# Making the low half of streamed weights with an accumulating transfer in the second mixer of a hybrid decoder trunk

## The chip, the cores and the metric

The kernel runs on one core of a Trainium2 chip. The metric is the device time of one launch in microseconds (us), lower is better. The engines of a core have one instruction queue each, worked off in order: TensorE (PE) multiplies matrices, VectorE (DVE) and ScalarE (ACT) work on 128 rows at a time, GpSimd (POOL) does small work, SyncE (SP) issues transfers. Transfers (DMA) run beside them on 16 engines. Waits between queues go over semaphores.

## The reference, cut to what matters

A trunk of two layers works on x of [1, 512, 1024] in float32. Each layer is a half feed-forward network, a mixer, and another half feed-forward network, each followed by a normalisation. The second layer's mixer, which the change touches, has RWKV-7 heads and gated linear attention (GLA) heads, one input projection and one output projection:

```python
def reference(x, ...):
    for l in range(DEPTH):                       # DEPTH = 2
        x = layer_norm(alpha * x + 0.5 * swiglu_ffn(x, ffn1_wi[l], ffn1_wo[l]), ...)
        mix = even_mixer(x, ...) if l % 2 == 0 else odd_mixer(x, ...)
        x = layer_norm(alpha * x + mix, ...)
        x = layer_norm(alpha * x + 0.5 * swiglu_ffn(x, ffn2_wi[l], ffn2_wo[l]), ...)

def odd_mixer(x, w_in, w_out, ...):
    p = x @ w_in
    y_rk = rwkv7_mixer(p[..., :RK_IN], ...)      # r, k, v, three small low-rank inputs
    y_gla = gla_mixer(*split_cols(p[..., RK_IN:], GLA_SIZES), ...)   # q, k, v, gate, output gate
    return jnp.concatenate([y_rk, y_gla], axis=-1) @ w_out

def rwkv7_mixer(p, ...):
    kk = heads(k * k_k)
    kk = kk / jnp.maximum(jnp.sqrt(jnp.sum(kk * kk, -1, keepdims=True)), 1e-12)   # the key norm
    def step(state, inp):                        # a scan over 512 tokens, 8 heads of 64
        sa = einsum(state, -kk_t)
        state = state * w_t + sa * (kk_t * a_t) + v_t * k_t
        return state, einsum(state, r_t)
    return (head_norm(y, ...) + (r * k * r_k).sum(-1) * v) * g
```

## The kernel before

**Three matmuls for one.** Every large product x @ w is made of three passes in a rounded 32-bit format (float32r): x is split into xh + xl and w into whi + wlo, and the kernel adds xh*whi, xl*whi and xh*wlo into one PSUM tile. In `project_T_steps` these are L122, L123 (the sixteen "high" matmuls of a chunk) and L126 (its eight "low" ones, after all high ones); in the GLA projections L146 to L148, in the feed-forward networks and the output projection L155 to L157.

**Streaming weights.** Weights come from HBM in chunks of 512 KB, a [128, 1024] float32 tile: 128 rows of 4 KB. `load` (L86) is SP's transfer into one of two `raw` tiles. `split` makes the halves in two pieces of 512 columns: ScalarE's copy rounds `raw` into `whi` (L98), VectorE subtracts: `wlo` = `raw` - `whi` (L100). There are five `whi` and five `wlo` tiles, taken in turn; a tile comes free when PE has read its last column of the chunk five earlier. `weights()` is called when a chunk's projection begins, splits up to two chunks ahead, and asks for two more loads.

**The second mixer** (`odd`) uses 34 chunks: a low-rank input and a gate, then twelve for k, r, v of four groups of heads (named k0, r0, v0, k1, ... below), four for the GLA q and k, four for v, four for the output gate, and eight for the output projection (`MixOut`). Its steps:

- k0, r0, v0 and the two small projections are made for the first 256 tokens; then the last quarter of x is transposed on PE (`pst`, L168) and the other 256 tokens follow.
- `keys` prepares a group of heads: a squared key (ScalarE, L690) summed by PE (`pn`), its floor on VectorE (L696), the power -0.5 on POOL (`nrm`, L697), a broadcast on ScalarE (L717), four transposes on PE (`pi`, L719), the scaled key on VectorE (L721) and products after it. VectorE's L744 masks the scores (`psc`) and ScalarE's L753 copies transposed keys (`KV`).
- `inverse` inverts 32 triangular blocks at a time by substitution: a chain of some sixty small VectorE operations (`ZU`, L782 and L783), ended by the 32x32 transposes L786 and L789. `merge` joins the blocks: PE's `pq` (L800) reads L786's result `WT`, ScalarE and VectorE copy `pq` (L802), PE's `px` (L807) reads that, L809 copies it, and `pwt`, `pu` (L822) follow. This comes twice, for head groups 0, 1 and 2, 3.
- The GLA heads' output gate `po` is scaled on VectorE by L958 and L959.

**What sets the order.** The program is written as Python that a scheduler reads: it simulates the engines, and puts each engine's instructions in the order of its own simulated times. Between the small steps, `fill()` takes matmuls of the projections that wait in a list (`filler`), as many as the table `FILL` gives for that place. An operation added or taken out in one place can so change the order on other engines.

## Time and profile before

| what | us |
|---|---|
| time, median of 3 runs | 2059.55 (2056.95 to 2061.2) |
| the profiled execution's own time | 2057.05 |
| its span (first to last instruction) | 2055.3 |
| TensorE busy | 2014.7 |
| VectorE busy | 1002.1 |
| ScalarE busy | 687.5 |
| GpSimd busy | 68.5 |
| mean granted TensorE clock | 0.983 |

Rows of the views are read so: in a group of instructions stand line, engine, operation, the tile written and the tiles read, shape and count, then the busy time with the mean in ns, then the engine's idle time just before and what ended most of it. A row of the timeline has its start, its length, engine, line, operation, tiles, shapes, count, and in brackets how long the engine stood idle before it and whose end released it. A window row has its bounds and length, then the busy time and count of each engine, the granted clock (1.00 is full), the busy share of the transfer engines, and GB/s. Matmuls overlap, so a matmul's length is more than the step from one to the next.

The second mixer lies between about 1329 and 1685 us. In the page's 40 slices of 51.4 us, TensorE is under nine tenths in four: two from 1387 to 1490 us, one from 1541 to 1593 us, and the last.

### The profile page before, as it was taken

The numbers are of one execution on the slowest core, as the hardware profiler recorded it, in microseconds if no ns is written. First come the engines' busy times: TensorE is split into PE (matmuls) and PEld (weight loads), VectorE is DVE, ScalarE is ACT, GpSimd is POOL, SyncE is SP. The second block draws the span as 40 slices with busy tenths as digits, with TensorE's granted clock in tenths as the row PEclk, the third lists the DMA queues.
The fourth block names the chain that finished last, engine by engine and source line by source line (L and its number), as shares of the span: only waits on it lengthen the run. The fifth ranks groups of instructions, "written<-read, shape, count | busy, mean of one in ns | idle before, by whom it ended". The sixth has DMA issues, their size and how long they took to land.

```text
span 2055.3 us, 26008 instructions
## 1 busy us (share of the span) xinstructions
PE 2014.7 (98%) x10485; PEld 1670.5 (81%) x10485; DVE 1002.1 (49%) x1858; ACT 687.5 (33%) x1206; POOL 68.5 (3%) x128
## 2 busy tenths in 40 slices
PE   9999999999999999999999999998898999999998
PEld 8888888977888888888888888886777688888886
DVE  4332333766783323336332333678758684323335
ACT  4331331556423322332332233255223334322330
POOL 0000000100010000000000000000010210000001
PEclk9999999999999999999999999998898999999999
DMA  5233332322233233332333333241113023333331
GB/s 176 93 102 113 103 93 82 107 92 62 66 100 113 92 102 114 101 95 72 113 92 103 113 98 97 86 140 40 59 31 114 1 74 119 95 97 118 94 102 62
DMA packets 56456, 191.42 MB, mean 93 GB/s; under 512 B 7488, under 2 KB 7952, under 8 KB 56336
## 3 DMA queue, kind: packets, MB, share of 16 engines
q1 hardware_dynamic: 56336, 189.77, 29.4%
q8 instruction: 82, 1.34, 0.3%
q14 instruction: 38, 0.31, 0.0%
HBM read 185.55 MB, written 4.19 MB: 92 GB/s over the span
## 4 chain that ended last, share of the span: by engine, by line
PE 90%; DVE 7%; ACT 1%; DMA 1%; issue 1%; POOL 0%; POOLq 0%; DVEq 0%; SPq 0%; ACTq 0%
PE pgu L122 16%; PE pgu L123 16%; PE pgu L126 16%; PE acc L157 8%; PE acc L155 8%; PE acc L156 8%; PE pout L155 1%; PE pout L156 1%; PE pout L157 1%; DVE wlo L100 1%; PE pj L122 1%; PE pj L123 1%; PE pj L126 1%; PE pst L168 1%; DVE ZU L782 1%; DVE ZU L783 1%
## 5 line engine op out<-in xcount | busy, mean ns | idle before, releaser
L100 DVE TENSOR_TENSOR wlo<-raw,whi 128x512 fp32r<-128x512 f32 x658 | 426.4, 686 | 549.6 <-ACT whi L98 513.2
L98 ACT ACTIVATE whi<-raw 128x512 fp32r<-128x512 f32 x661 | 379.6, 623 | 841.8 <-PE pgu L123 401.2
L122 PE MATMUL pgu<-xh,whi 128*128 128x512 f32 (+1 forms) x1568 | 563.1, 368 | 1.5 <-ACT whi L98 1.3
L123 PE MATMUL pgu<-xl,whi 128*128 128x512 f32 (+1 forms) x1568 | 564.0, 368 | 0.0
L126 PE MATMUL pgu<-xh,wlo 128*128 128x512 f32 (+1 forms) x1568 | 353.6, 367 | 0.0
L122 PEld LDWEIGHTS pgu<-xh,whi 128*128 128x128 f32 x1568 | 294.1, 188 | 50.4 <-ACT whi L98 1.5
L123 PEld LDWEIGHTS pgu<-xl,whi 128*128 128x128 f32 x1568 | 295.3, 189 | 48.6
L126 PEld LDWEIGHTS pgu<-xh,wlo 128*128 128x128 f32 x1568 | 275.8, 189 | 48.6
L155 PE MATMUL acc<-whi,hh 128*128 128x512 f32 x704 | 274.4, 390 | 0.0
L156 PE MATMUL acc<-whi,hl 128*128 128x512 f32 x704 | 274.2, 389 | 0.0
L157 PE MATMUL acc<-wlo,hh 128*128 128x512 f32 x704 | 272.3, 390 | 0.0
L233 DVE TENSOR_TENSOR sg<-sg,pgu 128x512 f32<-128x512 f32 (+1 forms) x96 | 61.6, 642 | 334.2 <-PE pgu L126 330.5
L156 PEld LDWEIGHTS acc<-whi,hl 128*128 128x128 f32 x704 | 132.2, 188 | 27.3
L157 PEld LDWEIGHTS acc<-wlo,hh 128*128 128x128 f32 x704 | 132.2, 188 | 27.2
L155 PEld LDWEIGHTS acc<-whi,hh 128*128 128x128 f32 x704 | 132.2, 188 | 27.0
L160 ACT ACTIVATE hh<-sg 128x512 fp32r<-128x512 f32 (+1 forms) x96 | 57.3, 597 | 120.9 <-DVE sg L233 120.9
L232 ACT ACTIVATE sg<-pgu 128x512 f32<-128x512 f32 (+1 forms) x96 | 53.7, 561 | 55.6 <-PE pgu L126 54.9
L160 ACT ACTIVATE xh<-pst 128x512 fp32r<-128x512 f32 x48 | 27.6, 598 | 108.5 <-PE pst L168 108.5
L122 PE MATMUL pj<-xh,whi 128*128 128x512 f32 (+2 forms) x184 | 63.5, 364 | 0.0
L190 POOL TENSOR_SCALAR rs<-mv 128x1 f32<-128x1 f32 x24 | 13.1, 547 | 1507.8 <-DVE mv L188 1507.8
L123 PE MATMUL pj<-xl,whi 128*128 128x512 f32 (+2 forms) x184 | 62.0, 354 | 0.0
L161 DVE TENSOR_TENSOR hl<-sg,hh 128x512 fp32r<-128x512 f32 (+1 forms) x96 | 61.5, 640 | 0.6 <-ACT hh L160 0.5
(336 smaller groups left out, 1968.6 us busy)
## 6 DMA issues: line engine op xcount, KB each, us to landing
raw<-ffn_wi SPq DMA_DIRECT2D x176, 512.0 KB, 3.5
raw<-ffn_wo SPq DMA_DIRECT2D x88, 512.0 KB, 3.5
raw<-od_krv SPq DMA_DIRECT2D x12, 512.0 KB, 3.5
raw<-ev_qk SPq DMA_DIRECT2D x8, 512.0 KB, 3.6
raw<-ev_rg SPq DMA_DIRECT2D x8, 512.0 KB, 3.5
raw<-ev_w_out SPq DMA_DIRECT2D x8, 512.0 KB, 3.5
raw<-od_w_out SPq DMA_DIRECT2D x8, 512.0 KB, 3.5
x<-x SPq DMA_DIRECT2D x4, 512.0 KB, 5.7
```

What stands on the lines that cost most here:

```text
L98: self.nc.scalar.activation(hi[:, sl], t[:, sl], AF.Copy)
L100: self.nc.vector.tensor_tensor(out=lo[:, sl], in0=t[:, sl], in1=hi[:, sl].bitcast(F32), op=ALU.subtract)
L122: mm(o, hi[:, kt, :n], self.xh[:, kt, t0:t1], start=kt == 0, stop=False)
L123: mm(o, hi[:, kt, :n], self.xl[:, kt, t0:t1], start=False, stop=lo is None and kt == 7)
L126: mm(o, lo[:, kt, :n], self.xh[:, kt, t0:t1], start=False, stop=kt == 7)
L155: mm(o, ah, hi[:, cs], start=first and i == 0, stop=False)
L156: mm(o, al, hi[:, cs], start=False, stop=False)
L157: mm(o, ah, lo[:, cs], start=False, stop=last and i == len(lhs) - 1)
L160: self.nc.scalar.activation(hi, src, AF.Copy)
L161: self.nc.vector.tensor_tensor(out=lo, in0=src, in1=hi.bitcast(F32), op=ALU.subtract)
L232: nc.scalar.activation(sg, pp[f, 0][:, t0:t1], AF.Silu)
L233: nc.vector.tensor_tensor(out=sg, in0=sg, in1=pp[u][:, t0:t1], op=ALU.mult)
```

## The change

From the start of `odd` until just before the mixer's last step, `split` makes `wlo` in another way. ScalarE makes two copies of each piece of 512 columns: the rounded `whi` as before, and `wlo` = -round(`raw`), a Copy with scale -1. POOL then issues a transfer that reads the chunk again from HBM and adds it to `wlo` in place (`accum_op`), so `wlo` = chunk - round(chunk), as before. SP's load into `raw` stays, since ScalarE reads it.

It holds for 29 chunks of this mixer: twelve of k, r, v, four each of GLA q and k, v, and output gate, and the first five of the output projection. The low-rank input was split before, the gate is of another kind (`fold`, its low part is packed in `whi`), and the last three of the output projection are split after the flag is off; these stay on VectorE. So 58 VectorE operations (L100) go, and 58 ScalarE operations and 29 transfers come.

```diff
--- before.py
+++ after.py
@@ -52,6 +52,7 @@
         self.srcs = []
         self.nl = self.nsp = self.nu = 0
         self.raw = {}
+        self.adds = False
         self.spl = {}
 
     def start(self):
@@ -84,20 +85,25 @@
         n = shape[0] * shape[1]
         t = self.wp.tile([P, 1024], F32, name="raw", bufs=NRAW)
         self.nc.sync.dma_start(t[:, :n].rearrange("p (a b) -> p a b", a=shape[0]), ap)
-        self.raw[self.nl] = (t, n, shape, fold)
+        self.raw[self.nl] = (t, n, shape, fold, ap)
         self.nl += 1
 
     def split(self):
         while self.nl <= self.nsp:
             self.load()
-        t, n, shape, fold = self.raw.pop(self.nsp)
+        t, n, shape, fold, ap = self.raw.pop(self.nsp)
         hi = self.wp.tile([P, 1024], F32R, name="whi", bufs=NSLOT)
         lo = None if fold else self.wp.tile([P, 1024], F32R, name="wlo", bufs=NSLOT)
         for z in range(0, n, 512):
             sl = slice(z, min(n, z + 512))
             self.nc.scalar.activation(hi[:, sl], t[:, sl], AF.Copy)
-            if not fold:
+            if self.adds and not fold:
+                self.nc.scalar.activation(lo[:, sl], t[:, sl], AF.Copy, scale=-1.0)
+            elif not fold:
                 self.nc.vector.tensor_tensor(out=lo[:, sl], in0=t[:, sl], in1=hi[:, sl].bitcast(F32), op=ALU.subtract)
+        if self.adds and not fold:
+
+            self.nc.gpsimd.dma_start(lo[:, :n].rearrange("p (a b) -> p a b", a=shape[0]), ap, accum_op=ALU.add)
         t, hi, lo = (z if z is None else z[:, :n].rearrange("p (a b) -> p a b", a=shape[0]) for z in (t, hi, lo))
         if fold:
             o = hi[:, :, fold:]
@@ -555,6 +561,7 @@
     def odd(self, l):
         nc, a, tc = self.nc, self.a, self.tc
         V, A, T, G = nc.vector, nc.scalar, nc.tensor, nc.gpsimd
+        self.adds = True
         xs = tc.alloc_tile_pool(name="xd", bufs=1, space=bass.MemoryType.DRAM).tile([S, D], F32, name="xs")
         for t in range(4):
             nc.sync.dma_start(xs[t * P:(t + 1) * P], self.x[:, t])
@@ -1100,6 +1107,7 @@
             for q in later:
                 rk_values(*q)
             gp.release()
+            self.adds = False
             mix.last(l, lambda nm: slot("y" if nm != "lnt" else "kr"))
 
 
```

The order moves with it. Line numbers of the changed kernel are one higher from L87 on, six higher after `split`, and seven higher in `odd`. On POOL, at the beginning of the mixer, before (`half`, `wk`: constants; `nrm`: the key norm):

```order
L191 TENSOR_TENSOR rs<-rs,expo 128x1
L587 MEMSET half 128x1
L620 MEMSET wk 80x512
L702 MEMSET wk 128x8
L697 TENSOR_TENSOR nrm<-nrm,expo 128x8
```

and now:

```order
L197 TENSOR_TENSOR rs<-rs,expo 128x1
L106 DMA wlo<-od_krv 128x1024
L594 MEMSET half 128x1
L106 DMA wlo<-od_krv 128x1024 x2
L627 MEMSET wk 80x512
L106 DMA wlo<-od_krv 128x1024 x3
L709 MEMSET wk 128x8
L106 DMA wlo<-od_krv 128x1024 x3
L704 TENSOR_TENSOR nrm<-nrm,expo 128x8
```

Nine transfers stand ahead of the first key norm, which had only constants before it.

On PE, the projections of the first 256 tokens, before (`pj_9945` is r0, `pj_9954` v0, `wlo_9920` the low part of r0; `pst` the transposes of x):

```order
L122 MATMUL pj_9945<-xh_71,whi_9919 128x256
L123 MATMUL pj_9945<-xl_72,whi_9919 128x256
L126 MATMUL pj_9945<-xh_71,wlo_9920 128x256 x4
L168 MATMUL pst_10067<-ident_73,x_70 128x128 x2
...
L168 MATMUL pst_10074<-ident_73,x_70 128x128 x4
L122 MATMUL pj_9954<-xh_71,whi_9928 128x256
```

and now (`pj_9939` and `wlo_9911` are k0, `pj_9949` r0, `pj_9959` v0):

```order
L128 MATMUL pj_9949<-xh_71,whi_9920 128x256
L129 MATMUL pj_9949<-xl_72,whi_9920 128x256
L174 MATMUL pst_10072<-ident_73,x_70 128x128 x4
L174 MATMUL pst_10079<-ident_73,x_70 128x128 x4
...
L128 MATMUL pj_9959<-xh_71,whi_9930 128x256
L129 MATMUL pj_9959<-xl_72,whi_9930 128x256
L132 MATMUL pj_9939<-xh_71,wlo_9911 128x256 x8
```

The transposes now stand among the high matmuls of r0, and k0's low matmuls, which came right behind its own high ones, stand behind half of v0's high ones. Those of r0 come later still, behind the second half of the low-rank projection.

On VectorE, the end of the second inverse, before (`og` is the output gate):

```order
L784 MEMSET ZU 64x32
L100 TENSOR_TENSOR wlo<-raw,whi 128x512
L783 TENSOR_TENSOR ZU<-ZU 64x2x29
...
L782 TENSOR_TENSOR ZU<-ZU 64x30
L958 SCALAR_TENSOR_TENSOR og_12118<-og_12118,po 128x512
L783 TENSOR_TENSOR ZU<-ZU 64x30
L959 TENSOR_TENSOR og_12118<-og_12118,cst 128x512
L786 STREAM_TRANSPOSE WT<-ZU 32x32x32
L789 STREAM_TRANSPOSE SC<-ZU 32x32x32 x2
L802 COPY WT<-pq 32x16x32
```

and now:

```order
L791 MEMSET ZU 64x32
L790 TENSOR_TENSOR ZU<-ZU 64x2x29
L789 TENSOR_TENSOR ZU<-ZU 64x30
L790 TENSOR_TENSOR ZU<-ZU 64x30
L793 STREAM_TRANSPOSE WT<-ZU 32x32x32
L796 STREAM_TRANSPOSE SC<-ZU 32x32x32 x2
L965 SCALAR_TENSOR_TENSOR og_12144<-og_12144,po 128x512
L966 TENSOR_TENSOR og_12144<-og_12144,cst 128x512
L809 COPY WT<-pq 32x16x32
```

No low part of weights is left in the chain of `ZU`, and the scaling of the output gate has moved behind the transposes.

## The prediction

> **What bounds the kernel now.** I read the page first: the span, TensorE's busy share and its 40 slices. Then the windows, cut where TensorE's idle time begins and ends, then the waits inside them.

> ```profile
> span 2055.3 us, 26008 instructions
> PE 2014.7 (98%) x10485; PEld 1670.5 (81%) x10485; DVE 1002.1 (49%) x1858; ACT 687.5 (33%) x1206; POOL 68.5 (3%) x128
> PE   9999999999999999999999999998898999999998
> L100 DVE TENSOR_TENSOR wlo<-raw,whi 128x512 fp32r<-128x512 f32 x658 | 426.4, 686 | 549.6 <-ACT whi L98 513.2
> q1 hardware_dynamic: 56336, 189.77, 29.4%
> raw<-od_krv SPq DMA_DIRECT2D x12, 512.0 KB, 3.5
> ```

> TensorE (PE) bounds the whole: 98% busy, and full in all slices but the last and three between 1387 and 1593 us (51.4 us each), which is the second mixer. The change touches only that mixer. The next rows are its stretches, all engines (us and count), then granted clock, DMA share and GB/s:

> ```profile
> 1331.00:1387.00 56.00, 56.00 (x369) 48.43 (x368) 40.47 (x72) 32.39 (x56) 3.70 (x8) 1.00 0.44 140
> 1387.00:1482.00 95.00, 82.69 (x635) 63.17 (x634) 76.79 (x140) 41.38 (x69) 5.76 (x7) 0.87 0.17 53
> 1533.00:1590.00 57.00, 49.88 (x450) 40.73 (x448) 46.50 (x93) 21.56 (x39) 1.07 (x4) 0.88 0.28 93
> ```

> The order is PE, weight loads, VectorE (DVE), ScalarE (ACT), GpSimd (POOL). In 1331-1387 PE never idles: whatever makes it wait there adds in full. In 1387-1482 PE idles 95.00-82.69 = 12.3 us, and VectorE is busy 76.79 of 95 us (81%). In 1533-1590 PE idles 7.1 us beside a VectorE that is 82% busy. In both, the clock is below full.

> Of VectorE's time, the low parts of weights (L100 alone, same stretches) take:

> ```profile
> 1387.00:1482.00 95.00, 11.79 (x18) 0.87 0.17 53
> 1533.00:1590.00 57.00, 8.13 (x12) 0.88 0.28 93
> ```

> **The change, term by term.** For 29 chunks of this mixer, 58 VectorE subtractions of 0.69 us go; 58 ScalarE copies and 29 accumulating transfers issued by POOL come. SP's loads stay.

> *Term 1, the first low parts (a loss).* The first three chunks (k0, r0, v0) arrive just before they are used, in the stretch where PE is full:

> ```profile
> 1332.14 2.38 ACT L98 ACTIVATE whi<-raw 128x512 fp32r<-128x512 f32 x4 [0.97 <-DMA raw<-od_krv]
> 1334.17 0.28 PE L122 MATMUL pj<-xh,whi 128*128 128x256 f32 x1
> 1334.29 0.28 PE L123 MATMUL pj<-xl,whi 128*128 128x256 f32 x1
> 1339.45 0.38 PE L168 MATMUL pst<-ident,x 128*128 128x128 f32 x2
> 1363.32 1.08 PE L126 MATMUL pj<-xh,wlo 128*128 128x512 f32 x4
> ```

> Four copies take 2.38 us. The two high and two negated ones of k0 are then done at 1332.14+2.38 = 1334.5 and its transfer can go. The new order reads k0's low part behind k0's and r0's high matmuls (16 each), 8 transposes and 8 high matmuls of v0: 40 x 0.12 (1334.29-1334.17) + 8 transposes at about 0.14 (two in under 0.38, less their overlap) = 5.9 us after 1334.17, so 1340.1. The transfer has 5.6 us.

> No row shows an accumulating transfer. The nearest is a plain load of the same 512 KB, 3.5 us: the lower bound. Splitting it: q1 is 29.4% of 16 engines x 2055.3 us over 56,336 packets = 0.172 us a packet; 128 rows of 4 KB are 8 packets an engine = 1.4 us of moving, so 2.1 us are fixed. Reading two operands makes the moving 2.8, reading and writing one after the other 4.2; with the fixed part 4.9 to 6.3, and POOL's issue, at most its slowest row below (1.65), makes 5 to 8. For the upper bound I double the slowest plain load:

> ```profile
> DMA to landing us min/median/max: 3.3/3.5/6.8
> ```

> 13.6 us. Against 5.6 us of room the cost is 0 (3.5) to +8 (13.6); a gain is excluded, since no PE wait is removed here. I take 7 us, nearest to the two-operand rows: 7 - 5.6 = 1.4, and **+2** with r0 and v0 behind it.

> [...]

> *Term 2, the key norm behind POOL's queue (a loss).*

> ```profile
> 1367.70 1.65 POOL L697 TENSOR_TENSOR nrm<-nrm,expo 128x8 f32<-128x8 f32 x1 [23.30 <-DVE nrm L696]
> 1369.38 0.63 ACT L717 ACTIVATE wk<-nrm 128x512 f32<-128x512 f32 x1 [1.48 <-POOL nrm L697]
> 1372.20 0.60 PE L719 MATMUL pi<-ident,wk 128*128 128x128 f32 x4
> 1389.40 1.98 PE L126 MATMUL pj<-xh,wlo 128*128 128x512 f32 x8
> ```

> In the new order POOL issues nine transfers ahead of this norm. The ninth waits for ScalarE's negated copy, that one for a low buffer (five of them), held until PE has read the fourth chunk's low part. From the fifth chunk's at 1363.32 PE has 8+15+11+8 = 42 matmuls at about 0.23 (1.98/8 with the overlap) and 4 small ones (1 us) to there: 1374.0. Then two copies 1.15, an issue of about 1, the norm 1.65, ScalarE's broadcast 0.63: 1378.4. PE reaches the waiting transposes (pi) 11 matmuls after that read, at 1376.5. So about 2 us, with 0.9 (issue free) to 4 (issue as long as the slowest POOL row, and term 1's delay added): **+2.5**. Queued behind pi on PE are the score matmuls of the first group, and on ScalarE, which waits at the broadcast, the next high parts.

> [...]

> *Term 3, the first VectorE-bound stretch (a gain).*

> ```profile
> 1391.47 1.29 DVE L100 TENSOR_TENSOR wlo<-raw,whi 128x512 fp32r<-128x512 f32 x2 [5.03 <-PE pj L126]
> 1395.33 1.33 PE L908 MATMUL pl<-ga,gw 80*128 80x512 f32 x2 [1.86 <-DVE wk L721]
> 1409.97 1.11 PE L752 MATMUL ptk<-ident,KRV 128*128 128x128 f32 x4 [1.39 <-DVE SC L744]
> 1426.55 0.97 PE L758 MATMUL ptb<-ident,bk 128*128 128x128 f32 x4 [1.61 <-ACT KV L753]
> 1475.01 1.76 PE L822 MATMUL pwt<-SC,KV 64*64 64x64 f32 x28 [2.70 <-DVE SC L809]
> 1445.36 1.98 PE L126 MATMUL pj<-xh,wlo 128*128 128x512 f32 x8
> ```

> VectorE stood 5.03 us behind a low part that waited for a buffer, with the scores' masks and L721 queued after it, and PE then waited for L721. That low part is first read at 1445.36, over 50 us later: the transfer is hidden here. VectorE gets 11.79 us of work and the 5.03 back. PE's idle time, 12.3 us, caps the gain, with a little clock above it. Waits on VectorE fall; the one on ScalarE (1.61) stays, and ScalarE gets 18 copies of about 0.57 (10 us), in a stretch where it is 44% busy. A bit over half of the cap: **-7** (-2 to -12). If ScalarE's copies stood ahead of its score copies the gain would end at -2.

> *Term 4, the end of the second inverse (a gain).*

> ```profile
> 1568.14 0.39 PE L148 MATMUL po<-wlo,xh 128*128 128x512 f32 x1
> 1573.32 1.81 PE L800 MATMUL pq<-WT,SC 32*32 32x32 f32 x64 [4.79 <-DVE WT L786]
> 1577.77 1.91 PE L807 MATMUL px<-SC,WT 32*32 32x32 f32 x62 [1.66 <-DVE WT L802]
> 1567.70 0.69 DVE L100 TENSOR_TENSOR wlo<-raw,whi 128x512 fp32r<-128x512 f32 x1
> 1570.55 0.69 DVE L959 TENSOR_TENSOR og<-og,cst 128x512 f32<-128x512 f32 x1
> 1571.28 1.90 DVE L786 STREAM_TRANSPOSE WT<-ZU 32x1024 f32<-32x1024 f32 x1
> 1577.02 0.69 DVE L802 COPY WT<-pq 32x512 f32<-32x512 f32 x1
> 1585.39 0.63 PE L148 MATMUL po<-wlo,xh 128*128 128x512 f32 x1
> 1585.82 0.63 PE L146 MATMUL po<-whi,xh 128*128 128x512 f32 x1
> ```

> PE waits 4.79 us for the transpose L786, the end of VectorE's substitution chain, into which ten of L100's twelve operations are laced (10 x 0.71 = 7.1 us), with the output scaling L958/L959 (1.4). All leave: L786 would come at 1571.28-8.5 = 1562.8, before PE's own filler ends at 1568.5. So pq starts at 1568.5 instead of 1573.32. The three transposes end at 1562.8+5.7 = 1568.5 too; the new order then puts the scaling (1.4) ahead of L802, so L802 runs at about 1570.8 and px at 1571.6 instead of 1577.77: -6. The matmuls here go at half pitch (0.43 between the last two rows, 0.23 elsewhere); a shorter gap gives back part of 12 x 0.2 = 2.4. **-7.5** (-3, if the fillers end as late as before and ScalarE's new copies hold the other half of WT, to -10).

> In 1482-1533 PE is nearly full, and after 1590 only two of the changed operations are left: 0, hidden behind PE.

> **Sum:** +2 + 2.5 - 7 - 7.5 = **-10 us**. The profiled execution took 2057.05 us, so 2047; it lies 2.5 under the median shown, 2059.55, on which basis I predict 2049.5.

> **The rivals.**
> *The transfers pace the start (slower).* Should the accumulating transfers run one behind the other at E us each, PE has five to read by 1363.32, from 1334.5: 28.8/5 = 5.8 us each. At E = 10 the fifth lands at 1384.5, 21 us late: +21+2.5-14.5 = +9, so 2068.5. It decides from 5E-28.8+2.5 = 14.5, E = 8.2. For it: no row shows this kind of transfer, and 13.6 is in bounds. Against it: moving 1.4 us, even three times, is far below. 0.13.
> *In-order waits eat the gains (a little slower).* POOL's later norms and ScalarE's copies stand behind transfers and buffers as in term 2; the 5.03 us wait moves to ScalarE, ahead of its projection copies. Three more waits like +2.5 and half of terms 3 and 4 (-7): +4.5+7.5-7, some +5, so 2064.5. For it: four key groups pass through POOL. Against: after the first, low buffers come free long before the norm. 0.10.
> *VectorE's time turns into other waits (no change).* ScalarE's score copies and PE's own order then set the pace: terms 3 and 4 give -3 each, +4.5 against: about -2, 2057.5. For it: waits on ScalarE stand between those on VectorE. 0.20.
> *More gain.* Both gaps close fully, with the clock back, and terms 1 and 2 cost nothing: -18, 2041.5. 0.05.

> **How the numbers follow.** The forecast, -16 to -4, has 0.52. A measurement tells 0.2% (4.1 us) from no change. Faster: 0.49 of the forecast, 0.05 of more gain, 0.03 of the no-change case = 0.57. Same: the other 0.17 and 0.02 of the forecast = 0.19. Slower: 0.13+0.10 and 0.01 over = 0.24. The range, 2037 to 2066, takes in more gain (beyond it terms 3 and 4 at their ends), no change and the in-order waits, and leaves out the pacing beyond +6.5; the forecast's own is 2043.5 to 2055.5.

> **What would show it.** Term 1: a wait of 1 to 3 us by PE for a DMA at k0's first low matmul, and POOL-issued transfers that land in 5 to 8 us. Term 2: the norm some 8 us later and a wait of pi for it. Term 3: no 5 us wait of VectorE near 1391, and PE idle some 5 to 6 us in the stretch that had 12.3. Term 4: PE's wait at pq under 1 us. Wrong if transfers land one after another more than 8 us apart, if PE's idle time in 1387-1482 stays over 10 us, or if ScalarE becomes the releaser of most PE waits.

## The result: faster, by more than forecast

The changed kernel took 2036.51 us (median of 4 runs, 2035.31 to 2039.38) beside 2059.5 for the kernel before: a ratio of 0.9893, 95% interval 0.9879 to 0.9907, 23 us faster. The forecast was 2049.5, its range 2037 to 2066; the time lies half a microsecond under it. The profiled execution took 2039.38 us, 17.7 less than that of before. A second series of the same kernel, below, was slower than the first (2046.26), and that is part of the explanation.

The page of the changed kernel, in the same parts as before:

```profile
span 2037.6 us, 26047 instructions
PE 2003.2 (98%) x10485; PEld 1661.1 (82%) x10485; DVE 966.1 (47%) x1800; ACT 716.7 (35%) x1264; POOL 95.1 (5%) x157
PE   9999999999999999999999999998999999999998
L103 DVE TENSOR_TENSOR wlo<-raw,whi 128x512 fp32r<-128x512 f32 x600 | 388.4, 687 | 533.4 <-ACT whi L99 507.8
q0 software_dynamic: 4176, 15.21, 4.0%
raw<-od_krv SPq DMA_DIRECT2D x12, 512.0 KB, 4.6
wlo<-od_krv POOLq DMA_DIRECT2D x12, 512.0 KB, 7.6
```

58 subtractions have left VectorE. The new transfers are the queue q0; those of k, r, v land 7.6 us after their issue in the median. PE has the same 10,485 matmuls, but is busy 11.5 us less, and its mean granted clock is 0.991 instead of 0.983: the same work ran at a higher clock.

**Where the time went.** I cut the mixer at five places of PE's program: the first low matmul of the projections (pj), the first of the GLA values (pv), the first of the output gate (po), the end of the last po that reads weights, the first of the output projection (pout). The windows, before and then changed (columns as in the prediction):

```profile
1331.33:1494.83 163.50, 151.16 (x1079) 120.53 (x1078) 123.03 (x233) 77.10 (x131) 11.12 (x18) 0.92 0.25 78
1494.83:1545.19 50.36, 48.84 (x298) 38.63 (x297) 31.93 (x92) 13.37 (x30) 6.38 (x16) 0.90 0.15 43
1545.19:1588.00 42.81, 35.69 (x343) 28.90 (x343) 33.81 (x68) 14.99 (x27) 0.00 (x0) 0.84 0.32 111
1588.00:1632.12 44.12, 40.03 (x433) 29.82 (x433) 29.91 (x105) 14.08 (x35) 8.35 (x20) 0.88 0.04 14
```

```profile
1330.94:1492.15 161.21, 149.52 (x1078) 119.11 (x1077) 97.81 (x193) 96.89 (x171) 29.92 (x38) 0.95 0.61 145
1492.15:1537.91 45.76, 44.23 (x297) 35.30 (x296) 28.12 (x87) 17.44 (x38) 8.66 (x16) 1.00 0.39 87
1537.91:1574.96 37.05, 35.29 (x343) 28.24 (x342) 27.56 (x57) 19.22 (x35) 4.50 (x8) 0.86 0.75 193
1574.96:1614.49 39.53, 35.86 (x434) 27.07 (x434) 29.37 (x103) 15.46 (x38) 9.23 (x21) 1.00 0.12 28
```

Call them stages 1 to 4. They changed by -2.3, -4.6, -5.8 and -4.6 us. Stages 1 and 3 hold everything that the forecast costed (terms 1 to 3, and 4): -8.1 against -10. Stages 2 and 4, which it put at zero, gave another -9.2. In both PE's idle time (length less busy) is about as before, 1.5 us in stage 2, and 4.1 and 3.7 us in stage 4; its clock is 1.00 where it was 0.90 and 0.88.

**What the clock does.** In stage 2 stands one and the same wait in both kernels:

```profile
1513.36 0.29 PE L840 MATMUL psa<-St,WT 128*64 128x128 f32 x1 [1.29 <-DVE St L852]
```

```profile
1510.68 0.29 PE L847 MATMUL psa<-St,WT 128*64 128x128 f32 x1 [1.29 <-DVE St L859]
```

Windows of PE alone around it, before and changed (length, PE busy, granted clock):

```profile
1512.07:1515.49 3.42, 2.13 (x18) 1.00 0.00 0
1515.49:1518.90 3.41, 3.41 (x18) 0.50 0.00 0
1518.90:1522.31 3.41, 3.41 (x21) 0.50 0.02 5
1522.31:1525.73 3.42, 3.42 (x11) 0.50 0.00 0
1525.73:1529.14 3.41, 3.41 (x25) 1.00 0.39 130
```

```profile
1506.74:1510.15 3.41, 2.65 (x16) 1.00 0.88 184
1510.15:1513.57 3.42, 2.89 (x21) 1.00 0.03 6
1513.57:1516.98 3.41, 3.41 (x35) 1.00 0.02 5
```

**What a half-clock field costs.** All executions of a kernel have the same instructions, yet 79 of the kernel before spread from 2050.6 to 2069.1 us, and their time follows their mean granted clock (correlation -0.89). Over all kernels here a clock lower by 0.001 goes with 1.61 us more; one field, half of 3.41 us at full clock lost, takes 1.71 of some 2056 us off the mean, 0.00083, so **1.34 us a field** on average (an estimate from these figures). Stage 2 shows it directly. PE idles 1.52 or 1.53 us in it in all seventeen traces, and its length is 45.7 to 45.8 us in the seven without a half-clock field, 48.8 in the two with two, 50.3 to 50.4 in the four with three, 51.9 in the four with four: 1.5 us a field where PE is otherwise busy, whatever the kernel. With the slope of 1.61 each kernel's mean difference to before splits into work and clock (us; an estimate, since one slope stands for all kernels):

| kernel | runs | mean us | mean clock | work | clock |
|---|---|---|---|---|---|
| before | 79 | 2058.5 | 0.982 | 0 | 0 |
| changed, first series | 4 | 2036.9 | 0.992 | -6.0 | -15.6 |
| changed, second series | 8 | 2044.7 | 0.988 | -4.6 | -9.1 |
| low parts from k1 on | 10 | 2036.9 | 0.991 | -8.4 | -13.2 |
| 17 later chunks | 10 | 2048.7 | 0.985 | -6.1 | -3.7 |
| nine k, r, v chunks | 10 | 2052.6 | 0.986 | +0.7 | -6.6 |
| six chunks of the second inverse | 10 | 2057.4 | 0.982 | -2.4 | +1.3 |
| no transfers | 9 | 2043.1 | 0.987 | -8.2 | -7.2 |

### The profile page after: what moved, and what is told of

It is laid out like the page before. It is cut to its first block, busy times and chain, and to the rows that moved or that the text cites. A ratio compares the mean times of both kernels' runs of the same rounds, so it can differ in the third digit from the quotient of the medians.

```text
span 2037.6 us, 26047 instructions
## 1 busy us (share of the span) xinstructions
PE 2003.2 (98%) x10485; PEld 1661.1 (82%) x10485; DVE 966.1 (47%) x1800; ACT 716.7 (35%) x1264; POOL 95.1 (5%) x157
## 3 DMA queue, kind: packets, MB, share of 16 engines
q1 hardware_dynamic: 56336, 189.77, 29.8%
q8 instruction: 82, 1.34, 0.3%
## 4 chain that ended last, share of the span: by engine, by line
PE 90%; DVE 4%; ACT 3%; DMA 2%; issue 1%; POOL 0%; POOLq 0%; SPq 0%; DVEq 0%; ACTq 0%
PE pgu L128 16%; PE pgu L129 16%; PE pgu L132 16%; PE acc L163 8%; PE acc L162 8%; PE acc L161 8%; PE pout L161 1%; PE pout L162 1%; PE pout L163 1%; DMA raw<-od_krv 1%; PE pv L152 1%; PE pst L174 1%; PE pj L128 1%; ACT whi L99 1%; PE pv L154 1%
## 5 line engine op out<-in xcount | busy, mean ns | idle before, releaser
L103 DVE TENSOR_TENSOR wlo<-raw,whi 128x512 fp32r<-128x512 f32 x600 | 388.4, 687 | 533.4 <-ACT whi L99 507.8
## 6 DMA issues: line engine op xcount, KB each, us to landing
raw<-ffn_wi SPq DMA_DIRECT2D x176, 512.0 KB, 3.5
raw<-ffn_wo SPq DMA_DIRECT2D x88, 512.0 KB, 3.5
raw<-od_krv SPq DMA_DIRECT2D x12, 512.0 KB, 4.6
wlo<-od_krv POOLq DMA_DIRECT2D x12, 512.0 KB, 7.6
raw<-ev_qk SPq DMA_DIRECT2D x8, 512.0 KB, 3.5
raw<-ev_rg SPq DMA_DIRECT2D x8, 512.0 KB, 3.4
raw<-ev_w_out SPq DMA_DIRECT2D x8, 512.0 KB, 3.5
raw<-od_w_out SPq DMA_DIRECT2D x8, 512.0 KB, 4.2
```

The source lines that it names most:

```text
L103: self.nc.vector.tensor_tensor(out=lo[:, sl], in0=t[:, sl], in1=hi[:, sl].bitcast(F32), op=ALU.subtract)
```

## The experiments

In the first, second and some later ones only the range of chunks changes for which the transfer is used (counted from the mixer's first chunk):

```diff
+        adds = self.adds and not fold and (self.nsp - self.base >= 5)
...
-            if self.adds and not fold:
+            if adds:
```

**The first three low parts on VectorE again** (range: 5 and up).

> The first three chunks (k0, r0, v0) get their low part from VectorE again; the other 26 keep the accumulating transfer. Theory S (the sum by stages: the mixer's beginning up to the k, r, v chunks' end lost 4.6 us, of which the late first low parts are a part): the wait of 2.1 us for k0's transfer and the half-clock window behind it go, so 3 to 5 us faster than the changed kernel, about 2032. Rival (the loss is the transfer engines' load and ScalarE's longer queue, which 26 chunks still bring): no change against the changed kernel, 2036 to 2038.

2034.17 us, ratio 0.9887 (0.9859 to 0.9916): between the two forecasts. Its first stage:

```profile
1333.87:1485.03 151.16, 144.36 (x1079) 115.87 (x1078) 101.28 (x199) 93.96 (x165) 26.49 (x35) 0.98 0.61 144
```

It is 10.1 us shorter than the changed kernel's, and PE idles 6.8 us in it instead of 11.7. A second series beside the changed kernel:

> The kernel with 26 chunks once more, beside the changed kernel on the same chip. Theory S: 2.5 us less than the changed kernel at the same clock (the wait for k0's transfer), 2034. Rival: no difference.

2040.37, 0.9907 (0.9872 to 0.9942), stage 1 at 155.8 us. At equal clock it is 2.4 to 3.8 us ahead of the changed kernel's two series; by the totals the intervals overlap. It is the best kernel of the study, as far as these runs tell.

**Only the 17 later chunks** (range: 14 and up).

> All twelve k, r, v chunks get their low part from VectorE again; the 17 later ones (GLA and output projection) keep the transfer. Theory S: the beginning is as before the change (4.6 us back), and the stages behind it keep their gains: 2031 to 2033. Rival V (the gain follows VectorE's removed operations one by one): 24 of 58 operations return, so about 24/58 of the 23 us are lost, 2046.

2049.54, 0.9956 (0.9938 to 0.9973). Neither forecast holds: the waits go as in theory S (work -6.1), the clock does not follow. Its trace is of its fastest execution, 2038.68 us at a clock of 0.989; the other nine took 2047.5 to 2051.9 at 0.983 to 0.985. The stages 1 and 4 of that trace:

```profile
1330.37:1483.82 153.45, 145.98 (x1079) 115.76 (x1078) 112.91 (x217) 85.30 (x147) 18.25 (x26) 0.97 0.42 111
1565.17:1613.47 48.30, 44.60 (x434) 32.78 (x434) 30.48 (x104) 15.65 (x38) 9.23 (x21) 0.79 0.11 23
```

Stage 1 is 10 us shorter than before without any transfer for k, r, v, so that stage's gain needs none of them; it comes with the later chunks that are split in it. How much of the 10 us this one execution owes to its clock is open: PE idles 7.5 us in the stage, against 9.1 to 12.4 in three traces of before, and the rest is clock. The nine later k, r, v transfers add nothing clear to it (151.2 and 155.8 above); the first three take most of it back (changed: 161.2).

**Only nine k, r, v chunks** (range: 5 to 13).

> Only nine of the k, r, v chunks (all but k0, r0, v0) use the transfer. If the parts add up, this is the rest of the kernel with 26 chunks (2034.2) without the 17 later ones (2049.5 against 2058.8): 2034.2 + 9.3 = 2043.5. By term 3 alone (its 7 us, without the clock): 2052. Rival (it is the order and not VectorE's time that changes the clock): anything, above all 2058 and more.

2052.23, 0.9968 (0.9951 to 0.9985). That is the number expected of term 3 alone, but not for its reason (work +0.7, clock -6.6). Its stages 1, 2 and 4:

```profile
1331.36:1499.59 168.23, 154.19 (x1079) 123.25 (x1078) 111.65 (x215) 85.72 (x149) 19.65 (x27) 0.90 0.38 104
1499.59:1545.36 45.77, 44.25 (x298) 35.29 (x297) 31.79 (x92) 13.37 (x30) 6.46 (x16) 1.00 0.15 47
1587.36:1626.55 39.19, 36.04 (x434) 27.21 (x434) 31.06 (x106) 14.66 (x36) 8.39 (x20) 1.00 0.05 15
```

The stage with the changed work is 4.7 us longer than before; the two without it are 4.6 and 4.9 shorter, at full clock. This kernel got faster where it was not changed.

**Only the six chunks of the second inverse** (range: 25 to 30).

> Only the six chunks whose low parts were laced into the second inverse (the last of the output gate and five of the output projection) use the transfer; all others are VectorE's. Theory S: the whole gain of the second inverse, term 4 with its clock, comes from these: 8 to 11 us faster than before, about 2049, and the same as with all 17 later chunks (2049.5). Rival V (the gain follows the number of removed operations): 12/58 of 23 us, 2054.

2058.27, 0.9994 (0.9975 to 1.0012): no change, so neither theory's total. Its stages 3 and 4 (the trace is of the slowest of ten executions, 2061.86 us):

```profile
1548.57:1584.50 35.93, 34.02 (x343) 27.44 (x343) 27.56 (x57) 19.04 (x35) 4.58 (x8) 0.90 0.76 198
1584.50:1636.99 52.49, 47.74 (x434) 34.96 (x434) 29.87 (x103) 15.67 (x38) 9.31 (x21) 0.74 0.10 22
```

Stage 3 gave 6.9 us, near the 7.5 of term 4; in this trace stage 4 took 8.4 back, with eight half-clock fields instead of three.

**The transfers left out** (the low part stays -round(raw)).

```diff
-            self.nc.gpsimd.dma_start(lo[:, :n].rearrange("p (a b) -> p a b", a=shape[0]), ap, accum_op=ALU.add)
+            pass
```

> The transfers are left out, so the low part of 29 chunks is only -round(raw) and the result is another one; ScalarE's 58 copies and the freed VectorE stay. It measures the transfers' own cost in the changed kernel. Theory S: the 2.1 us wait for k0 and POOL's held norm go, 3 to 5 us faster than the changed kernel, about 2032. Rival (the transfers cost nothing, the beginning's loss is ScalarE's): 2036 to 2037.

2043.4, 0.9927 (0.9904 to 0.9951): no faster than the changed kernel in total, 2 to 4 us faster in work. Stage 1 is 152.4 us against 161.2 (PE's order, without the transfers' simulated time, is another there): with the two series of the first experiment that puts the price of the transfers, of the first three above all, at 5 to 10 us of stage 1, of which 3 to 6 us are PE's idle time and the rest clock.

**A shift ahead of the mixer**, in the kernel before and in the changed one:

```diff
         o = ps[:n, t0:t1]
+        if self.nu == 180:
+            for _ in range(8): mm(o, self.xh[:, 0, :n], self.xh[:, 0, t0:t1], start=True, stop=True)
```

> The kernel before with eight extra matmuls (1.84 us at 0.23) in the feed-forward network ahead of the mixer; TensorE's order stays the same up to the second inverse. Theory K (the half-clock windows fall where a gap meets a fixed window grid, so much of the gain is which windows are hit): the eighteen half-clock windows of 3.41 us in the mixer move or change in number, and the time differs from 2059.5 + 1.8 by 3 us or more either way. Rival (the clock only follows the gaps, wherever they lie): 2061.3 within 1.5 us, and the same stretches at half clock, 1.8 us later.

2052.91 (2050.55 to 2056.65), 0.9985 (0.9969 to 1.0001), an interval that just takes in no change. By the means, split as in the table, eight matmuls of 0.23 us of extra work went with 5.1 us less time (+0.8 of work, -5.9 of clock), as theory K allows; its trace has no half-clock field in stages 2 and 4.

> The changed kernel with the eight extra matmuls (1.84 us) ahead of the mixer that the kernel before also got; the order of TensorE stays the same up to the merge of the second inverse and a few dozen instructions are exchanged behind it. Theory L (the order behind the second inverse is a lottery for the clock, and the changed kernel drew well): the time moves by clearly more than 1.8 us and the clock with it, 2042 or more. Rival (the gain in the clock follows from VectorE's removed work): 2037 + 1.8 = 2039, clock 0.992.

2046.18, 0.9943 (0.992 to 0.9967), clock 0.989: theory L's number. But the unshifted kernel, measured beside it in the next experiment, took 2046.26, so the shift itself changed nothing that these series can tell. In its trace the wait in stage 2 lay within a field, and two half-clock fields followed.

**The changed kernel again.**

> The changed kernel once more, unaltered, for how far its own executions spread. Theory K (each execution meets the 3.41 us grid of the clock elsewhere, but the gaps in its order decide how many half-clock windows it can have): mean 2037, clock 0.991 to 0.993 in nearly all, within 5 us. Rival (its first four executions met the grid luckily): a spread like the kernel before's, 2033 to 2050, and clocks down to 0.985.

2046.26 us (2037.77 to 2049.82), 0.993 (0.9906 to 0.9954): the rival was right (it had 2033 to 2050). Three of its eight executions have a clock of 0.990 or 0.991 and 2037.8 to 2042.3 us, five 0.986 or 0.987 and 2045.6 to 2049.8. Its trace (2045.59) against the first one: stages 1 to 3 agree within 1.5 us, stage 4 is 48.2 us instead of 39.5:

```profile
1574.41:1577.82 3.41, 2.80 (x76) 1.00 0.49 121
1577.82:1581.23 3.41, 3.41 (x34) 0.50 1.00 183
1581.23:1584.65 3.42, 3.42 (x23) 0.50 0.03 6
1584.65:1588.06 3.41, 2.47 (x17) 0.50 0.00 0
1588.06:1591.47 3.41, 3.41 (x27) 0.50 0.02 5
1591.47:1594.89 3.42, 3.42 (x31) 0.50 0.00 0
1594.89:1598.30 3.41, 3.41 (x26) 0.50 0.00 0
```

A field with PE busy 2.80 of 3.41 us was followed by six at half clock, one of them with a further wait in it, where the first trace had 2.91 of 3.42 in the emptiest field of that place and none followed. The later series ran on four different chips, on which the kernel before had medians of 2055.9 to 2058.8 us; for the first series the chip is not recorded, so a part of the difference between the two may be the chip's and not chance. A single execution of the changed kernel on another of the four, below, took 2036.76.

**PE's waits filled with matmuls** whose results are overwritten, in the second inverse, without (before) and with 26 transfers. `warm` is (14, 5, 12) and (0, 5, 8): the first number goes ahead of `pq`, the second ahead of `px`, the third behind the first matmul of `px`:

```diff
                 p = self.psum("pq", "C")
+                for _ in range(warm[0]):
+                    T.matmul(p, self.xh[:, 0, :P], self.xh[:, 0], start=True, stop=True)
...
                 p = self.psum("px", "C")
                 for m in range(32):
+                    if m < 2:
+                        for _ in range(warm[1 + m]):
+                            T.matmul(p[0:32, 256:512], self.xh[:, 0, :32], self.xh[:, 0, :256], start=True, stop=True)
```

> The kernel before, with matmuls whose results are overwritten put into the second inverse's waits of TensorE: 14 of 512 columns and 5 of 256 ahead of pq, 12 of 256 inside px. In the order the output gate's scaling also moves behind the transposes on VectorE (1.4 us). Theory K (a window of 3.41 us in which TensorE is busy under about 0.75 puts the next windows at half clock, and each of these costs about 1.4 us): the four half-clock windows behind the second inverse go, so 5 to 7 us faster than before, about 2052, and no half-clock window between the inverse and 1590 us. Rival (the half clock there costs nothing, since PE waits anyway): at best the 1.4 us, 2057 to 2060.

2056.77, 0.9984 (0.9966 to 1.0002), where the rival had 2057 to 2060. One half-clock field is left of four behind the inverse and stage 3 is 40.2 us instead of 42.8, but stage 4 has four fields instead of three. The 6 us are not there.

> The kernel with 26 chunks (2034.2) and overwritten matmuls in the second inverse's px: 5 of 256 columns before it, 8 inside, 1.6 us in waits of 0.7 and 1.1 us. Theory K: the window behind which the clock fell (busy 0.54) is filled, the three half-clock windows there go, and about 4 us with them: 2030. Rival: no gain, 2034 to 2035.

2042.75, 0.9918 (0.9891 to 0.9945): no faster than without (2034.17 and 2040.37). Stages 3 and 4:

```profile
1538.27:1571.20 32.93, 32.70 (x356) 26.37 (x356) 26.89 (x56) 19.15 (x35) 4.51 (x8) 1.00 0.82 217
1571.20:1620.53 49.33, 43.42 (x433) 31.83 (x433) 29.67 (x103) 15.12 (x37) 9.24 (x21) 0.83 0.11 23
```

In its place it went as forecast: the three fields are gone, and stage 3 fell by 4.1 us (37.0 without the filling). Stage 4, whose VectorE order moved, lost 9.6.

**The first inverse's waits filled** (5 matmuls ahead of pq, 12 ahead of the first pwt).

> The kernel before, with overwritten matmuls at the first inverse: 5 of 512 columns ahead of pq, 12 ahead of the first pwt. In the order, VectorE's low parts and key products that stood between the first inverse's merge steps move behind them; no operation leaves VectorE. Theory G (the four half-clock windows that follow the wait of pwt near 1475 us are the part of the clock gain that the change brings for good): they go without any transfer, 4 x 1.3 us, and with them the 2.7 us of the wait, less some 3 us of extra matmuls: about 2054, clock 0.985 to 0.986. Rival (only taking work off VectorE does it): 2059 to 2062.

2052.95, 0.9981 (0.9966 to 0.9995), clock 0.986. The total fits theory G, the trace only half: two fields at the first inverse instead of four, and stage 1 no shorter (164.9 us). What this trace gained is stage 4 without a field (39.2 us against 44.1).

**Both kernels traced again.**

> The kernel before, unaltered, for one more trace. Theory G: four half-clock windows (13.65 us) begin near 1471 to 1478 us again; those near 1515 (three) and 1600 us (three) may be there or not. Rival: the windows near 1475 come and go as well.

> As the look before: four half-clock windows near 1475 by theory G, the others by chance.

> The changed kernel, unaltered, for one more trace. Theory G: one window behind k0's wait near 1342 us, none between 1430 and 1500 us, and two to nine between 1560 and 1600 us by chance. Rival: windows between 1445 and 1500 us here too.

2063.16, 2057.31 and 2036.76 us. Half-clock fields by place, in the three traces of each kernel:

| place | before | changed |
|---|---|---|
| k0's transfer, 1342 us | 0, 0, 0 | 1, 1, 0 |
| first key groups, 1385-1435 | 4, 6, 3 | 4, 4, 4 |
| first inverse, 1465-1485 | 4, 5, 4 | 0, 0, 0 |
| stage 2, 1515 | 3, 3, 3 | 0, 0, 0 |
| second inverse and stage 4, 1560-1625 | 7, 12, 7 | 3, 8, 3 |
| sum | 18, 26, 17 | 8, 13, 7 |

Theory G holds for the first inverse: four or five fields in each trace of before, none in those of the change (its shifted copy has one, at 1477.5). The field behind k0's wait, which it expected in the last trace, is not there.

## Why the prediction missed

The direction was right, and most of the waits moved as forecast; the size was not: -10 was forecast, the first series gave -23, and the second -11.4 (2046.26 against 2057.7, the median of its own 15 runs of before). That the first series fell out of the range is in part luck, and so is the second one's nearness: by the table above the work gave only -6.0 and -4.6, and the clock, to which the forecast gave a little in terms 3 and 4 and nothing elsewhere, -15.6 and -9.1.

- **Term 1 (+2), right in its wait.** PE waited 2.09 us for k0's transfer, which it reached at 1339.8 (forecast 1340.1):

```profile
1341.91 1.29 PE L132 MATMUL pj<-xh,wlo 128*128 128x256 f32 x8 [2.09 <-DMA wlo<-od_krv]
DMA to landing us min/median/max: 6.1/7.3/10.8
```

  The second line is of all 29 transfers. That of k0 took 7.6 us, about the 7 chosen. q0's 4.0% of 16 engines over 29 transfers is 2.8 us of moving each (an estimate from the page's line), as the two-operand case had it. What was not in the term: a half-clock field behind the wait, in two of three traces (PE was busy 1.32 of the 3.41 us before it).
- **Term 2 (+2.5), right in place, small in size.** The norm began at 1378.8 us, 11 us later than before (some 8 were forecast; the issue of about 1 us in that sum was an estimate that no row of before shows, and the 29 issues took 0.85 to 1.08 us), pi waited 0.84 us, and behind it stand waits that were not forecast: pw 2.2 and pa 1.6 us. With the first three low parts on VectorE those of k0, pi and pw are all gone (pa's stays), so term 2 too hangs on the first three transfers. Terms 1 and 2 together: stage 1 is 160.4 us in the mean of three traces of the changed kernel, 153.5 in the mean of the two with those three on VectorE: +7, where +4.5 stood. Of the 7, 4.2 us are PE's idle time and the rest is clock.
- **Term 3 (-7), right in sign, its size not settled.** Without the k, r, v transfers stage 1 falls from 163.8 (mean of three) to 153.5 in the one trace there is, of a fast execution: -10, of which 3.8 us are PE's idle time and the rest is clock, above all the four or five half-clock fields of the first inverse. The range's end was -12. Of the eighteen low parts that the term counts, sixteen are of GLA chunks, and with nine of the k, r, v chunks alone the stage did not get shorter (168.2). One sign failed: VectorE's wait of 5.03 us did not go but stands at 1383 us with 5.63, behind a ScalarE that waited 2.38 us for the late norm.
- **Term 4 (-7.5), right.** Stage 3: 43.0 to 36.6 us in the means of three traces, -6.4. Before pq there is no wait any more (4.79 us before); px still waits:

```profile
1563.07 0.24 PE L814 MATMUL px<-SC,WT 32*32 32x32 f32 x2 [0.68 <-ACT WT L809]
1564.39 1.68 PE L814 MATMUL px<-SC,WT 32*32 32x32 f32 x62 [1.08 <-DVE WT L809]
```

- **"In 1482-1533 ... and after 1590 ...: 0", the step that failed.** These are stages 2 and 4: -4.6 and -3.6 in the means of three traces, together nearly as much as the whole forecast. Their work and their waits are about what they were; the half-clock fields in them are fewer, three to none in stage 2, and 3, 7, 3 to 0, 6, 0 in stage 4. The windows of before showed a clock below full there (0.87 and 0.93):

```profile
1482.00:1533.00 51.00, 49.46 (x310) 37.73 (x310) 26.88 (x92) 12.30 (x29) 6.97 (x16) 0.87 0.11 32
1590.00:1665.00 75.00, 70.36 (x556) 53.58 (x555) 51.40 (x172) 23.32 (x60) 14.26 (x33) 0.93 0.12 36
```

  I read that as a property of the stage, when it was the echo of single waits (1.29 us in stage 2, 0.94 us ahead of the three fields in stage 4). In stage 2 the echo is there or not by where the wait falls on the grid; for stage 4 that was not sorted out. "PE is nearly full" was no reason for a zero: a full PE ran at half clock here (busy 3.41 of 3.41 us at 0.50 from 1515.49 us on).
- **The range.** Its lower end, 12.5 us under the forecast, took "more gain" as both gaps closed. Executions of the kernel before alone spread over 18 us, and the medians of the changed kernel's two series lie 9.8 us apart; the range made no allowance for that.

Whether stage 2 is free of fields in the changed kernel by its order or by luck stays open: three of three traces are, but its shifted copy is not, and the wait itself is unchanged. By the places above, a wait that falls anywhere on the grid goes without fields in about three cases of ten (an estimate: 0.93 to 1.11 of 3.41 us), so three of three would be rare as luck, if the three are independent of each other, which no run shows. The same holds for the two outcomes of stage 4. What is shown is that the fields make the difference in these two stages (PE's idle time changed by under half a microsecond); that the change removes them for good is not.

## What to carry to other kernels

Sum waits on TensorE, and then count the fields of the clock's grid that follow each of them: here 1.3 to 1.5 us for a field, and two to four fields after a wait of 1.3 us where it falls badly, so that such a wait cost 3 to 6 us more (stage 2: 45.7 to 45.8 us without a field, 48.8 to 51.9 with two to four), and also where the edit touched nothing (nine k, r, v chunks: stages 2 and 4 went without fields and were 4.6 and 4.9 us shorter). Where that is so, PE's idle time stage by stage, with the fields counted apart from it, tells what the edit did; a median of four executions does not. And of the work moved to a transfer, here only that paid which stood in the way of a busy engine's chain and had time to land: the seventeen later chunks gave the gain in work (-6.1), the first three, of which k0's was wanted 5.5 us after its transfer began, cost (stage 1 is 7 us longer with them).

## What was not expected of the hardware

Recovery was slow here: with PE busy all through (3.41 of 3.41 us, as from 1515.49 us on before), the clock stayed at half for two to four fields after one emptier field in stage 2, and for up to eight in stage 4, where further waits lie between. And the busy share does not decide alone: in one trace of the changed kernel a field busy 0.82 was followed by six at half clock, while in stage 2 of the same trace one busy 0.66 (2.26 of 3.41 us) was followed by none. Nor is 0.75, as in theory K, a border: in the trace of before one busy 0.69 (2.36 of 3.41 us, at 1460.88) was followed by full clock, one busy 0.79 (2.69 of 3.42 us, at 1467.70) by half. POOL's issue of an accumulating transfer is shown with 0.85 to 1.08 us in all 29 cases, also in those where VectorE was busy throughout (as at 1387.6 us); what stood behind one on POOL began as little as 0.53 us after its start (a constant at 1388.14 behind the issue at 1387.61; the norm at 1378.77 followed 0.57 us behind the one at 1378.20). The twelve of k, r, v:

```profile
L106 POOL DMA_DIRECT2D wlo<-od_krv x12: 862/869/1077, 1334.3 to 1404.4; - x12
```
